# Seven products for eight in the query and forget projections of a recurrence, with the sums on GpSimd

## The chip, the core and the metric

The kernel runs on one core of one Trainium2 chip. Its engines work side by side: TensorE (PE: matrix products, with its weight loads shown apart as PEld), VectorE (DVE), ScalarE (ACT), GpSimd (POOL) and SyncE (SP, which here issues DMAs). Each executes its own instructions in the order in which they were written down, and waits for others by semaphores. SBUF is the memory of 128 partitions that they share; PSUM holds what TensorE sums, in banks of 128x512 float32. The metric is the device time of one execution, in microseconds (us).

## The reference

A decoder trunk of two layers, for 1024 tokens of width 1024, all in float32. The first layer mixes tokens by a gated linear recurrence with 8 heads of width 128; the change lies in it.

```python
q, f, i, g = jnp.split(h @ w_in, 4, axis=-1)
fg = lb + (1.0 - lb) * jax.nn.sigmoid(heads(f))
o = hgrn2_chunkwise(jax.nn.silu(heads(q)), 1.0 - fg, heads(i), jnp.log(fg))
o = o * lax.rsqrt(jnp.mean(jnp.square(o), -1, keepdims=True) + RMS_EPS)
o = o * g_norm_w.astype(jnp.float32) * jax.nn.silu(heads(g))
return o.reshape(B, S, D).astype(h.dtype) @ w_out
```

Behind it come a layer norm with the residual, a gated FFN (width 2816, a causal convolution of width 3), another norm; then the second layer with sliding-window attention in place of the recurrence, and its FFN.

## The kernel before

**Products in three parts.** Matrices are split into a high part, rounded to the format fp32r, and a low part, the rest; each product of a 128-row chunk is the sum of three matmuls of 128x512 (high x high, high x low, low x high; `mm3`, lines 194 to 196). `T` holds x transposed, high and low, 8 chunks `kc` of 128 rows by 1024 tokens. `HL` holds weights in high and low parts, 12 buffers of 1024 columns. A split is a cast on ACT (line 176) and a subtraction on DVE (line 169).

**The stages.** Up to 37.5 us x is loaded, transposed and split, and the i and g projection of head 0 is computed (lines 752, 714, 715). Then the heads follow. For each, the query and forget projection (`qf`: 4 slots, forget and query for the first 512 and the last 512 tokens, 8 chunks x 3 matmuls each, into one bank of PSUM that is read when it is full) is followed by the i and g projection (`ig_block`: 8 token blocks, 16 matmuls each). Between these matmuls stand those of the recurrence of the head before: for widths 256, 128, ... 8, DVE multiplies decays into `qp` (line 990) and `kp` (line 992) and goes on with the products of decays `tot` (line 995), and TensorE sums scores and column sums from them (line 200); ACT copies (lines 971, 977, 978, 1048, 1058). DVE's line 1184 computes, whenever the plan finds it free, differences of blocks of the FFN's down-projection weights: those two products are computed with seven block products for eight already, and their sums are stored to DRAM (`bsd`) from the buffer `Y`. The finished heads are kept in `Y` as well. From about 430 us the heads are moved to `T`, and the out projection, the norm and the FFN follow.

**What sets the order.** The recurrence stage is written out by hand for all engines. `Order` counts planned time of TensorE (`od.t`) and DVE (`od.v`). Chains of small tasks (`spawn`, `later`) are due at times of that plan: at each `tick` behind a chunk product, what is due is emitted. `lay` fills DVE's gaps: due low parts of splits, then block sums, then moves. `slot_begin` loads and stores the block sums' rows.

**Buffers.** Weights of the heads come through a ring of three raw buffers; `Y` (32 KB of each partition) serves x, block sums, heads, and later the FFN.

## Time and profile before

| | |
|---|---|
| runs (3), median | 2131.06 us (2130.61 to 2131.86) |
| profiled execution | 2131.04 us, span 2129.3 us |
| PE busy | 2119.9 us, 100% |
| DVE busy | 1760.9 us, 83% |
| ACT busy | 926.5 us, 44% |
| POOL busy | 132.5 us, 6% |
| HBM read / written | 213.94 MB / 62.94 MB |
| heads, 60 to 430 us: DMA | busy share 0.44, 152 GB/s |

A row of instructions gives line, engine, operation, output<-inputs by the program's names, the shape in partitions x elements, and a count; behind the bar stand busy time and the mean of one in ns, then the idle time of the engine just before them and who ended it. A row of a timeline starts with start and duration in us; neighbours that are alike are put together, with their count behind an x. PE's matmuls are pipelined: their durations overlap, so the spacing of starts tells what one costs.

### The profile page before, as it was taken

The numbers are of one execution on the slowest core, as the hardware profiler recorded it, in microseconds if no ns is written. First come the engines' busy times: TensorE is split into PE (matmuls) and PEld (weight loads), VectorE is DVE, ScalarE is ACT, GpSimd is POOL, SyncE is SP. The second block draws the span as 40 slices with busy tenths as digits, with TensorE's granted clock in tenths as the row PEclk, the third lists the DMA queues.
The fourth block names the chain that finished last, engine by engine and source line by source line (L and its number), as shares of the span: only waits on it lengthen the run. The fifth ranks groups of instructions, "written<-read, shape, count | busy, mean of one in ns | idle before, by whom it ended". The sixth has DMA issues, their size and how long they took to land.

```text
span 2129.3 us, 32129 instructions
## 1 busy us (share of the span) xinstructions
PE 2119.9 (100%) x12663; PEld 1779.6 (84%) x12663; DVE 1760.9 (83%) x2375; ACT 926.5 (44%) x1491; POOL 132.5 (6%) x150
## 2 busy tenths in 40 slices
PE   9999999999999999999999999999999999999998
PEld 8888888888888888888888888888888888888887
DVE  4777776677999999887988658969999999978986
ACT  4444444452444444434433356743544444444430
POOL 1000000001100000000001113321000000000002
PEclk9999999999999999999999999999999999999999
DMA  5655443214223222228854411042233222249662
GB/s 216 243 211 169 144 132 119 75 32 177 99 85 98 85 89 79 80 99 275 288 190 161 129 26 45 24 149 89 80 100 98 90 86 83 86 148 325 229 215 90
DMA packets 229838, 278.96 MB, mean 131 GB/s; under 512 B 29960, under 2 KB 158648, under 8 KB 226872
## 3 DMA queue, kind: packets, MB, share of 16 engines
q1 hardware_dynamic: 228736, 276.53, 39.0%
q8 instruction: 99, 1.62, 0.3%
q10 hardware_dynamic: 856, 0.37, 0.1%
q14 instruction: 51, 0.42, 0.1%
q0 software_dynamic: 96, 0.02, 0.0%
HBM read 213.94 MB, written 62.94 MB: 130 GB/s over the span
## 4 chain that ended last, share of the span: by engine, by line
PE 99%; DMA 0%; DVE 0%; SPq 0%; issue 0%; DVEq 0%
PE psmm L194 17%; PE psmm L196 17%; PE psmm L195 17%; PE psax L194 10%; PE psax L196 10%; PE psax L195 10%; PE psmm L714 5%; PE psax L200 4%; PE psmm L715 3%; PE psmm L204 1%; PE psmm L200 1%; PE psax L204 1%; PE psax L1427 1%; PE psmm L1274 1%; DMA Y<-in_x_dram 0%; PE psmm L752 0%
## 5 line engine op out<-in xcount | busy, mean ns | idle before, releaser
L194 PE MATMUL psmm<-T,HL 128*128 128x512 f32 x768 | 303.4, 395 | 0.0
L196 PE MATMUL psmm<-T,HL 128*128 128x512 f32 x768 | 299.4, 390 | 0.0
L195 PE MATMUL psmm<-T,HL 128*128 128x512 f32 x768 | 299.2, 390 | 0.0
L473 DVE SCALAR_TENSOR_TENSOR Y<-Y,cwt 128x1023 f32<-128x1023 f32 (+1 forms) x176 | 225.0, 1281 | 44.3 <-ACT Y L471 42.9
L221 ACT CAST HL<-rx 128x1024 fp32r<-128x1024 f32 (+1 forms) x151 | 150.7, 1007 | 178.3 <-PE psmm L195 30.9
L169 DVE TENSOR_TENSOR HL<-rx,HL 128x1024 fp32r<-128x1024 f32 (+1 forms) x151 | 178.5, 1188 | 16.9 <-ACT HL L221 16.8
L714 PE MATMUL psmm<-HL,T 128*128 128x512 f32 x496 | 176.8, 399 | 0.0
L196 PEld LDWEIGHTS psmm<-T,HL 128*128 128x128 f32 x768 | 144.2, 188 | 30.7
L194 PEld LDWEIGHTS psmm<-T,HL 128*128 128x128 f32 x768 | 144.3, 188 | 29.6 <-issue 0.4
L195 PEld LDWEIGHTS psmm<-T,HL 128*128 128x128 f32 x768 | 144.3, 188 | 28.8 <-issue 0.4
L471 ACT ACTIVATE Y<-Y,cwt 128x1024 f32<-128x1024 f32 x88 | 108.7, 1238 | 101.6 <-DVE Y L460 89.4
L715 PE MATMUL psmm<-HL,T 128*128 128x256 f32 x496 | 138.9, 280 | 0.0
L194 PE MATMUL psax<-T,HL 128*128 128x512 f32 x352 | 137.3, 390 | 0.0
L196 PE MATMUL psax<-T,HL 128*128 128x512 f32 x352 | 137.0, 389 | 0.0
L195 PE MATMUL psax<-T,HL 128*128 128x512 f32 x352 | 137.0, 389 | 0.0
L243 POOL TENSOR_TENSOR rs<-rs,nhalf 128x1 f32<-128x1 f32 x32 | 44.6, 1394 | 1286.6 <-DVE rs L242 1286.6
L714 PEld LDWEIGHTS psmm<-HL,T 128*128 128x128 f32 x496 | 93.1, 188 | 21.0
L715 PEld LDWEIGHTS psmm<-HL,T 128*128 128x128 f32 x496 | 93.7, 189 | 0.4
L221 ACT CAST HT<-rx 128x1024 fp32r<-128x1024 f32 (+1 forms) x37 | 35.5, 960 | 127.9 <-DVE rx L427 76.4
L169 DVE TENSOR_TENSOR HL<-raw,HL 128x1024 fp32r<-128x1024 f32 x51 | 62.1, 1219 | 20.2 <-ACT HL L176 19.3
L195 PEld LDWEIGHTS psax<-T,HL 128*128 128x128 f32 x352 | 66.2, 188 | 13.7
L196 PEld LDWEIGHTS psax<-T,HL 128*128 128x128 f32 x352 | 66.1, 188 | 13.6
(315 smaller groups left out, 5232.3 us busy)
## 6 DMA issues: line engine op xcount, KB each, us to landing
rx<-in_ffn_w_in_dram SPq DMA_DIRECT2D x136, 256.0 KB, 3.2
rx<-gd SPq DMA_DIRECT2D x118, 256.0 KB, 3.9
Y<-in_ffn_w_out_dram SPq DMA_DIRECT2D x44, 512.0 KB, 6.4
bsd<-Y SPq DMA_DIRECT2D x22, 1024.0 KB, 4.8
gd<-Y SPq DMA_DIRECT2D x44, 512.0 KB, 2.6
rx<-in_ffn_w_out_dram SPq DMA_DIRECT2D x54, 256.0 KB, 4.7
R<-bsd SPq DMA_DIRECT2D x44, 256.0 KB, 5.1
Y<-in_ffn_w_in_dram SPq DMA_DIRECT2D x40, 256.0 KB, 2.9
```

What stands on the lines that cost most here:

```text
L169: make = lambda e: e.tensor_tensor(lo, src, hi.bitcast(F32), op=ALU.subtract)
L194: nc.tensor.matmul(ps, st(0), mv(0), start=start, stop=False)
L195: nc.tensor.matmul(ps, st(0), mv(1), start=False, stop=False)
L196: nc.tensor.matmul(ps, st(1), mv(0), start=False, stop=stop)
L200: nc.tensor.matmul(ps, lhsT, rhs, start=start, stop=stop, **kw)
L204: nc.tensor.transpose(ps, src, ident)
L221: nc.scalar.copy(hi, src)
L243: nc.gpsimd.tensor_tensor(rs, rs, nhalf, op=ALU.pow)
L471: nc.scalar.activation(c, u, AF.Identity, bias=cwt[:, l, 3, ci:ci + 1], scale=cwt[:, l, 2, ci:ci + 1])
L473: nc.vector.scalar_tensor_tensor(c[:, sh:], u[:, :S - sh], cwt[:, l, 2 - sh, ci:ci + 1], c[:, sh:], op0=ALU.mult, op1=ALU.add)
L714: nc.tensor.matmul(ps, T[:, 0, kc, ts], w[:, :, kc % 4, :], start=kc == 0, stop=False)
L715: nc.tensor.matmul(ps[:, :256], T[:, 1, kc, ts], w[:, 0, kc % 4, :], start=False, stop=kc == KC - 1)
```

## The change

**Seven products for eight.** Of the 8 chunks of x, the first four are treated as 2x2 blocks: early and late tokens (512 each) by chunks 0-1 and 2-3. The weights are blocks of chunks 0-1 and 2-3 by query and forget. Their product takes seven block products, with four sums of x blocks and four of weights. Chunks 4 to 7 are multiplied as before. In `T`, the late tokens of chunks 0 and 1 now hold the sum of the late blocks; a new buffer `Sx` holds three more sums, high and low. Per head 90 matmuls of 128x512 stand in place of 96. Since `T` is no longer plain x there, the i and g projection takes weight differences (`us[2]`) for chunks 2 and 3 of late tokens.

**Where sums are made.** The weights' sums (line 696: four of 128x256 a head; line 685: one of 128x512), three of the four sums of x blocks at the start (lines 831 to 841, 16 operations) and the block sums of the FFN weights (line 1329, before line 1184 on DVE) run on GpSimd. The block sums go in halves of 256 columns through a new buffer `Yx`, in two chains 7.5 us apart by the plan; a load, 7 us, four differences, 4 us, a store.

**Banks.** Products that several results share stay in PSUM: the bank `pa` gets query early, forget early, forget late and query late one after the other, `pc` forget late and forget early. What stands in a bank is copied by ACT (lines 1034, 1041, 1044) or added by DVE (line 1000), and then TensorE adds to the same bank.

**Outputs through DRAM.** `Y` is allocated behind the heads now. Heads 0 to 5 are stored to `hod` and loaded into `Sx` during head 7's projection; head 6 goes to `Yx`. The out projection takes the late tokens first. Two raw buffers hold loads, the third the sums. Transposes of constants wait while a projection has all banks.

```diff
@@ qf
-            for half in range(2):
-                ts = slice(half * 512, (half + 1) * 512)
-                ps = psmm()
-                proj_T(weights["f"], half, ps)
-                nc.scalar.activation(fg[:, ts], ps, AF.Sigmoid)
...
-                proj_T(weights["q"], half, ps)
-                nc.scalar.activation(qs[:, ts], ps, AF.Sigmoid)
...
+            q, f, e = [weights[g] for g in "qfe"]
+            early, late = slice(0, 512), slice(512, 1024)
...
+            def add_on(ps, w, w0, mv, n, start=False, stop=True):
+                for k in range(n):
+                    for j, (wi, mi) in enumerate(((0, 0), (0, 1), (1, 0))):
+                        nc.tensor.matmul(ps, w[:, wi, w0 + k, :], mv(mi, k), start=start and k + j == 0,
+                                         stop=stop and k == n - 1 and j == 2, skip_group_check=True)
...
+            def plus(ts, ps):
+                nc.vector.tensor_tensor(fg[:, ts], fg[:, ts], ps, op=ALU.add)
...
+            def third(ps):
+                plus(late, ps)
...
+            pa = psmm()
+            add_on(pa, q, 0, tokens(early), 2, start=True)
+            nc.scalar.copy(qs[:, early], pa)
+            ps = psmm()
+            add_on(ps, q, 2, tokens(early, 2), 6, start=True)
+            after(1.0, query_early(ps))
+            del ps
+            yield
+            add_on(pa, e, 2, sums(0), 2)
+            nc.scalar.copy(fg[:, early], pa)
+            pc = psmm()
+            add_on(pc, f, 0, tokens(late), 2, start=True)
+            nc.scalar.copy(fg[:, late], pc)
+            pd = psmm()
+            add_on(pd, f, 4, tokens(late, 4), 4, start=True)
+            yield
+            add_on(pa, e, 0, sums(1), 2)
+            after(0.5, third(pa))
+            add_on(pc, f, 4, tokens(early, 4), 4, stop=False)
+            after(0.0, forget_late(pd))
+            del pd
+            yield
+            add_on(pc, f, 2, sums(2), 2)
+            after(0.5, forget_early(pc))
+            del pc
+            od.finish(mine[1:2])
+            add_on(pa, e, 4, tokens(late, 2), 2, stop=False)
+            add_on(pa, q, 4, tokens(late, 4), 4)
+            od.finish(mine)
+            nc.scalar.activation(qs[:, late], pa, AF.Sigmoid)
+            nc.vector.tensor_tensor(qs[:, late], qs[:, late], pa, op=ALU.mult)
@@ sums of weights
+        sub2 = nc.gpsimd.tensor_tensor
+        def ig_diff(raw):
+            d = tail["raw"][2][:, :512]
+            sub2(d, raw[:, 512:], raw[:, :512], op=ALU.subtract)
...
+        def qf_sums(q, f):
+            b11, b21, b12, b22 = q[:, :256], q[:, 256:512], f[:, :256], f[:, 256:512]
+            t3, t2, t4 = [tail["raw"][2][:, 256 * i:256 * (i + 1)] for i in range(3)]
+            for x, y, z in ((t3, b22, b12), (b12, b12, b11), (t2, b22, b12), (t4, b21, t2)):
+                sub2(x, y, z, op=ALU.subtract)
@@ block sums of the FFN weights
-                for x, y, z in ((b11, b12, b11), (b12, b22, b12), (b22, b22, b11), (b21, b21, b22)):
-                    pending.append(lambda x=x, y=y, z=z: tt(x, y, z, op=sub))
...
+            while halves:
+                i, j = halves.pop(0)
+                l, n = divmod(i, pairs)
                 for k in range(2):
+                    row = (k * pairs + n) * P
+                    nc.sync.dma_start(rows[k], part(a["ffn_w_out"][l][row:row + P, :], j))
+                yield 7.0
                 for x, y, z in ((b11, b12, b11), (b12, b22, b12), (b22, b22, b11), (b21, b21, b22)):
+                    sub2(x, y, z, op=ALU.subtract)
+                yield 4.0
+                for k in range(2):
+                    nc.sync.dma_start(part(bsd[l][:, n, k, :], j), rows[k])
+                yield 4.0
@@ heads' outputs
-            if h < NH - 1:
-                nc.scalar.activation(Y[:, h, :], ps, AF.Copy, scale=par[:, 16:17])
+            if h < NH - 2:
+                flat = og.rearrange("p c t -> p (c t)")
+                nc.scalar.activation(flat, ps, AF.Copy, scale=par[:, 16:17])
+                del ps
+                yield 2.0
+                nc.sync.dma_start(hod[:, h, :], flat)
```

**The order at the changed places.** First TensorE in the query and forget projection of head 0, which has no recurrence beside it. Before, at the change from the first slot's bank to the second's (a number behind a name tells one buffer from another):

```order
L194 MATMUL psmm_460<-T_81,HL_83 128x512
L195 MATMUL psmm_460<-T_81,HL_83 128x512
L196 MATMUL psmm_460<-T_81,HL_83 128x512
L194 MATMUL psmm_490<-T_81,HL_83 128x512
L195 MATMUL psmm_490<-T_81,HL_83 128x512
L196 MATMUL psmm_490<-T_81,HL_83 128x512
```

Each bank was filled by 24 matmuls in a row and then left. The whole projection now, where psmm_518 is `pa` and psmm_555 is `pc`:

```order
L989 MATMUL psmm_518<-T_81,HL_82 128x512 x6
L989 MATMUL psmm_528<-T_81,HL_82 128x512 x18
L989 MATMUL psmm_518<-Sx_102,HL_82 128x512 x6
L989 MATMUL psmm_555<-T_81,HL_82 128x512 x6
L989 MATMUL psmm_570<-T_81,HL_82 128x512 x12
L989 MATMUL psmm_518<-Sx_102,HL_82 128x512 x6
L989 MATMUL psmm_555<-T_81,HL_82 128x512 x12
L989 MATMUL psmm_555<-Sx_102,HL_82 128x512 x6
L989 MATMUL psmm_518<-T_81,HL_82 128x512 x18
```

The bank of the first six is entered again three times, psmm_555 once, each time behind 18 matmuls into others.

Then ScalarE in such a projection, with the recurrence of the head before beside it. Before, head 3:

```order
L900 ACTIVATE fg<-psmm 128x512
L901 ACTIVATE fg<-fg,lbt 128x512
L903 ACTIVATE kp<-fg,one 128x512
L977 COPY kd<-qp 128x32x16
L978 COPY kd<-kp 128x32x16
L907 ACTIVATE qs<-psmm 128x512
L176 CAST HL<-raw_100 128x1024
L977 COPY kd<-qp 128x8x64
```

And now, head 4, where lines 1125 and 1126 are the old 977 and 978:

```order
L1034 COPY qs<-psmm 128x512
L719 ACTIVATE sg<-VG 128x256
L1125 COPY kd<-qp 128x32x16
L1126 COPY kd<-kp 128x32x16
L1041 COPY fg<-psmm 128x512
L1013 ACTIVATE kp<-qs 128x512
L1044 COPY fg<-psmm 128x512
L1125 COPY kd<-qp 128x8x64
```

Copies out of PSUM stand where sigmoids stood, and the recurrence's copies between them as before.

Last GpSimd in the heads. Before, its rows from the start to the norm of the first head (lines 1099 and 1100, which then come once a head):

```order
L793 DMA pr<-in_hgrn_lb_logits_dram 16x128
L794 DMA pr<-in_hgrn_gnorm_w_dram 1x16x8
L169 TENSOR_TENSOR HL<-raw_99,HL 128x1024
L1099 TENSOR_SCALAR ss<-ss 128x8
L1100 TENSOR_TENSOR ss<-ss,nhalf 128x8
```

Now, from the norm of one of the last heads on (the raw buffers are raw_99 to raw_101):

```order
L1247 TENSOR_SCALAR ss<-ss 128x8
L1248 TENSOR_TENSOR ss<-ss,nhalf 128x8
L1329 TENSOR_TENSOR Yx<-Yx 128x256 x8
L696 TENSOR_TENSOR raw_101<-raw_99 128x256
L696 TENSOR_TENSOR raw_99<-raw_99,raw_100 128x256
L696 TENSOR_TENSOR raw_101<-raw_99 128x256
L696 TENSOR_TENSOR raw_101<-raw_100,raw_101 128x256
L1329 TENSOR_TENSOR Yx<-Yx 128x256 x8
L685 TENSOR_TENSOR raw_101<-raw_99 128x512
L1329 TENSOR_TENSOR Yx<-Yx 128x256 x8
```

The differences of both chains of block sums stand in groups of eight, and between them those of the projection weights.

343 lines of the change are left out of this document (215 added, 128 removed).

## The prediction

> **What bounds the kernel now.** I read the page's busy table and slices first, then the chain that ended last, then the busy time by stage, then single instructions around the work that changes.
>
> ```profile
> PE 2119.9 (100%) x12663; PEld 1779.6 (84%) x12663; DVE 1760.9 (83%) x2375; ACT 926.5 (44%) x1491; POOL 132.5 (6%) x150
> PEclk9999999999999999999999999999999999999999
> PE 99%; DMA 0%; DVE 0%; SPq 0%; issue 0%; DVEq 0%
> ```
>
> ```profile
> 0.00:37.50 37.50, 35.80 (x233) 32.74 (x234) 17.43 (x31) 16.34 (x27) 6.16 (x14) 1.00 0.57 197
> 37.50:60.00 22.50, 22.50 (x101) 18.62 (x100) 10.49 (x15) 8.93 (x13) 0.00 (x0) 1.00 0.76 277
> 60.00:430.00 370.00, 370.00 (x3817) 315.23 (x3817) 266.45 (x490) 164.61 (x370) 13.13 (x14) 1.00 0.44 152
> ```
>
> TensorE (PE) is busy for 2119.9 of the span of 2129.3 us, and the chain that ended last is PE for 99%. The second fence has one row per stretch: its length, then busy time of PE, weight loads, VectorE (DVE), ScalarE (ACT) and GpSimd (POOL), the granted clock, the DMA share and GB/s. The changed work lies in the first three stretches and the 65 us behind them. From 37.5 to 430 us PE has no idle time at all, at a clock of 1.00. So each matmul taken away there is worth its full spacing, and each wait of PE that the change makes costs its full length. DVE has 266 of 370 us of work there, ACT 165, POOL 13.
>
> **What the matmuls are worth.** These rows are of one slot of a query and forget projection; between are ten more rows, lines 194, 195 and 196 in turn.
>
> ```profile
> 301.06 0.39 PE L194 MATMUL psmm<-T,HL 128*128 128x512 f32 x1
> ...
> 303.56 0.39 PE L196 MATMUL psmm<-T,HL 128*128 128x512 f32 x1
> ```
>
> The twelve starts span 2.50 us, eleven steps of 0.227 us (the 0.39 us is latency and overlaps). Per head the two projections had 4 x 8 chunk products of 3 matmuls, 96. Of the eight block products over the first four chunks, two chunks each, one is replaced by sums; 30 chunk products are left, 90 matmuls. 8 heads x 6 = 48 matmuls fewer, and no other count on PE changes: 48 x 0.227 = **-10.9 us**. The i and g projections use other weights for the late tokens but as many matmuls. As PE was never idle there, nothing that the change removes from DVE is a further gain.
>
> **Work taken from DVE.** The sums of weight blocks for the down projection move from DVE to POOL.
>
> ```profile
> L1184 DVE TENSOR_TENSOR Y<-Y 128x512 f32<-128x512 f32 x80 | 54.6, 690 | 1.3
> L990 DVE TENSOR_TENSOR qp<-qp,tot 128x512 f32<-128x512 f32 x42 | 28.9, 688 | 25.6 <-PE psax L200 25.4
> L992 DVE TENSOR_TENSOR kp<-kp,tot 128x512 f32<-128x512 f32 x42 | 28.8, 686 | 0.0
> ```
>
> (80 of the 88 lie in this window.) 88 x 0.69 = 60.7 us leave DVE; some 35 us come back: 32 operations of 128x512 more behind the projections (additions from PSUM, line 1000, above all), 22 us, and 8 low halves of 128x768 and 8 of 128x512 of the summed weights, 13 us. DVE then works about 240 us in the 359 that are left of the stretch. That is off PE's path, cost 0; it buys the slack that is used below.
>
> **Work put on POOL.** There are 176 differences of 128x256 of the block sums, 32 of the projection weights, 8 differences of 128x512 for i and g, and 16 sums of x at the start. The nearest rows:
>
> ```profile
> L1447 POOL TENSOR_TENSOR X<-X,bf 128x512 f32<-128x512 f32 x32 | 41.1, 1286 | 54.4 <-DVE X L1439 52.6
> L478 POOL TENSOR_TENSOR Y<-Y 128x1024 f32<-128x1024 f32 x4 | 9.6, 2399 | 100.3 <-DVE Y L473 100.3
> ```
>
> 512 elements more cost 1.11 us, so 128x256 is estimated at 1286 - 557 = 0.73 us. In the heads POOL gets 208 x 0.73 + 8 x 1.29 = 162 us, 45% of the stretch; it fits. The two streams of block sums fall together in the order, so POOL runs bursts of eight, 5.8 us, about 22 times. What POOL does to DVE meanwhile is in the next rows, two pairs from the FFN:
>
> ```profile
> 606.46 2.39 POOL L478 TENSOR_TENSOR Y<-Y 128x1024 f32<-128x1024 f32 x1 [44.25 <-DVE Y L473]
> ```
> ```profile
> 606.75 2.65 DVE L428 TENSOR_TENSOR rx<-rx,Y 128x512 f32<-128x512 f32 x1
> ```
> ```profile
> L428 DVE TENSOR_TENSOR rx<-rx,Y x20: 683/686/2646, 606.8 to 1866.6; 128x512 f32<-128x512 f32 x20
> ```
> ```profile
> 1269.97 1.29 POOL L1447 TENSOR_TENSOR X<-X,bf 128x512 f32<-128x512 f32 x1
> ```
> ```profile
> 1270.36 1.28 DVE L1470 TENSOR_TENSOR Y<-psmm,tri 128x512 f32<-128x512 f32 x2
> ```
> ```profile
> L1470 DVE TENSOR_TENSOR Y<-psmm,tri x32: 674/681/692, 1259.8 to 1407.4; 128x512 f32<-128x512 f32 x32
> ```
>
> A DVE operation with both inputs in SBUF, begun 0.29 us into POOL's, took 2.65 us against a median of 0.69: it stood still until POOL was through at 608.85. The two with one input in PSUM ran in their usual time beside POOL. So each two-SBUF operation of DVE that meets a POOL difference loses up to 0.73 us. Whether that reaches PE is a question of slack, read at one step of the recurrence:
>
> ```profile
> 295.15 0.69 DVE L990 TENSOR_TENSOR qp<-qp,tot 128x512 f32<-128x512 f32 x1
> 295.75 0.69 DVE L992 TENSOR_TENSOR kp<-kp,tot 128x512 f32<-128x512 f32 x1
> ...
> 297.50 1.44 DVE L1184 TENSOR_TENSOR Y<-Y 128x512 f32<-128x512 f32 x2
> 299.68 0.69 DVE L990 TENSOR_TENSOR qp<-qp,tot 128x512 f32<-128x512 f32 x1 [0.73 <-PE psax L200]
> ```
> ```profile
> 298.97 0.67 PE L200 MATMUL psax<-qp,kp 128*32 128x32 f32 x31
> ```
>
> PE's scores of qp and kp start at 298.97; the L992 that they need ended at 296.44: 2.53 us of slack. Blocked twice (L990, L992) DVE is 1.46 us late, three times 2.19, both hidden; four times 2.92, and PE waits 0.4. In between L990 waits for PE anyway (25.6 us over 42, 0.6 each), and the L1184s are gone, two of them 1.44 us here; both pay lateness back. So most bursts should be covered. Bounds: 0, or a whole 0.73 us in each of 22 bursts, 16 us. Nearest to the step shown, where two or three blocks stay inside the slack, I take +0.1 us a burst: **+2 us**. If the cover is gone, the PE scores are late next, and with them everything behind them in PE's order.
>
> **Banks that PE enters again.** In a projection one bank of PSUM (pa, lines 1032 to 1063) holds four results one after the other and another (pc) two; ACT copies out what stands there (lines 1034, 1041, 1044), and once DVE adds it (line 1000), before PE goes on in the same bank. Between lie 18 matmuls of another bank, 18 x 0.227 = 4.1 us, four times a head. Before, no bank was needed again so soon. The lags from the end of a bank to its copy, as they stand before:
>
> ```profile
> 200.32 0.39 PE L196 MATMUL psmm<-T,HL 128*128 128x512 f32 x1
> ```
> ```profile
> 200.75 0.60 ACT L907 ACTIVATE qs<-psmm 128x512 f32<-128x512 f32 x1 [3.66 <-PE psmm L196]
> ```
> ```profile
> 133.92 0.39 PE L196 MATMUL psmm<-T,HL 128*128 128x512 f32 x1
> ```
> ```profile
> 138.13 1.65 ACT L1048 COPY A<-Ab 32x256 f32<-32x256 f32 x4
> 139.79 0.60 ACT L900 ACTIVATE fg<-psmm 128x512 f32<-128x512 f32 x1
> ```
> ```profile
> 302.45 0.68 DVE L910 TENSOR_TENSOR qs<-qs,psmm 128x512 f32<-128x512 f32 x1
> ```
> ```profile
> 296.72 0.39 PE L196 MATMUL psmm<-T,HL 128*128 128x512 f32 x1
> ```
>
> Normal is 0.20 us after the spacing of the last matmul (200.55 to 200.75). At the worst ACT came 5.64 us late (134.15 to 139.79), behind copies that wait for DVE, and DVE's read came 5.50 late (296.95 to 302.45) behind two updates. A copy of 0.6 us and a handover of 0.2 leave 3.3 us of the 4.1 for lag. The worst ACT case would cost 2.3, the DVE case 2.2. Bounds: 0, and two ACT cases and three DVE cases, 11 us. The order of the changed kernel has at most two DVE-bound copies ahead of an evacuation on ACT, and DVE's line 1000 right behind the update of width 32, with the L1184s gone: nearer to the 0.20 row. I take **+2 us**, about one late bank.
>
> **The start.** Four token blocks get sums of x before their split, 16 operations on POOL, with 4 + 1 + 4 x 0.7 us of weights: about 4 x 1.29 + 12 x 0.73 + 1.29 + 2.9 = 18 us on an engine that had 6 busy in 37.5. What PE needs soonest, the sum for the two leading chunks, is one addition on DVE and doesn't wait for POOL; the other sums are read only after the first 24 matmuls of the first projection, at 37.55 + 24 x 0.227 = 43 us. DVE had 17.4 busy, so there is room, but blocks by POOL may fall on the path. Bounds 0 and 1.7 (PE's idle time of this stretch once more); I take **+0.5**.
>
> **Edits at nothing.** The finished heads go to DRAM and back, 6 stores of 512 KB and 3 loads of 1 MB, during heads 0 to 5 and head 7: the DMA share there is 0.44, and the loads are issued a projection ahead of use. The weight rows come in 256 KB pieces, and each store of sums on SP waits for POOL; weight loads of the next head stand behind it in that queue, and they are issued one to two slots (5.4 us each) before they are split. If POOL is late by a burst of 5.8 us this cover just holds. The out projection takes the late tokens first, with the same matmuls. The constants' transposes move by a few us. Each 0, bounded by 1 us together either way.
>
> **Sum.** -10.9 + 2 + 2 + 0.5 = -6.4. The profiled execution took 2131.04 us (span 2129.3), the median of the runs 2131.06: 2131.04 - 6.4 = **2124.6 us**, 0.30% faster. About 0.2%, 4.3 us, is what a measurement of this kernel can tell from no change.
>
> **Rivals.**
>
> *All waits hidden.* For it: the slacks above, and DVE's idle time of 100 us in the heads. Against: four new re-entries a head, and POOL from 13 to 160 us. 2131.04 - 10.9 = 2120.1, to 2122.
>
> *GpSimd blocks DVE past its slack; this ends slower.* Place: the scores behind L1138 and L1140 (the old L990 and L992) while a burst of eight runs. It decides once four blocked operations come in a row without an idle gap, since 4 x 0.73 is more than 2.53. For it: with POOL and DVE in turn, DVE runs at half speed for a burst of 10 us, and low halves and gates stand between the updates. Price 0.73 us or more a burst, 16 to 22 us: 2131.04 - 10.9 + 2.5 + 16 = 2138.6.
>
> *GpSimd keeps DVE out for a whole group.* If POOL's next difference goes ahead of the waiting DVE operation, DVE stands 5.8 us and PE 5.8 - 2.5 = 3.3; at half of the bursts 36 us: 2158.6. Against: all but the first difference of a group wait for the one ahead of them, so POOL lets go between. The row at 606.75 shows one POOL operation only, so the trace does not exclude it. The Trainium skill, SBUF — State Buffer, § Who interferes with whom, says that whichever of the two starts first holds the shared pair for the whole instruction and the other fully blocks; by that, a hold ends with each instruction, which speaks for turns and for 2124.6 rather than for 2158.6. That the block lasts to the end of POOL's operation agrees with 606.75 (2.65 us); who gets the pair next no run here shows.
>
> *Late banks.* All five late cases of before come back, at 2.2 each: 2131.04 - 10.9 + 0.5 + 2 + 11 = 2133.6, no change that can be told.
>
> **Chances.** My forecast, 2122 to 2127: 0.30; all hidden 0.27; GpSimd past the slack 0.20; kept out for groups 0.10; late banks 0.13. Faster takes the first two, 0.57; same takes late banks and the milder end of the third, 0.18; slower 0.25. The range 2119.8 to 2141 leaves out the group case and the far end of the third; the forecast's own range is 2122 to 2127.
>
> **What would show it.** PE's spacing stays 0.227 us and its matmuls fall by 48. POOL's differences take 0.7 us and DVE operations with two SBUF inputs beside them up to 1.4. The waits of PE, 1.5 us before, name DVE or ACT behind lines 1034 to 1044 and 1000 (banks, 2 us) or lines 1138 and 1140 (blocks, 2 us). I am wrong if PE's waits sum to more than 7 us, if they lie at the start or the out projection, or if POOL's 128x256 takes far from 0.73.

## The result and the profile after

The changed kernel takes 2196.57 us, median of 4 runs (2193.35 to 2197.38), beside 2131.36 (2130.61 to 2131.86) for the kernel before on the same chip: a ratio of 1.0303, 95% interval 1.0286 to 1.0321. It is 65 us slower. The forecast was 2124.6 us, with a range up to 2141: wrong in sign and far outside.

The busy table and the chain that ended last, after the change:

```profile
PE 2132.0 (97%) x12615; PEld 1780.9 (81%) x12615; DVE 1804.7 (82%) x2351; ACT 952.0 (43%) x1547; POOL 368.1 (17%) x382
...
PE 84%; DVE 9%; ACT 3%; DMA 1%; issue 1%; POOL 1%; SPq 0%; DVEq 0%; ACTq 0%; POOLq 0%
```

The 48 matmuls are gone (12663 to 12615), and yet PE is busy 12.1 us longer. In a span of 2194.7 us it stands idle for 62.7, where it stood idle for 9.4 (2129.3 - 2119.9). So the account closes in three terms: waits +53.3, matmuls not issued -10.9, and +23.0 of longer busy time of the others (12.1 + 10.9); together +65.4, the difference of the spans. The chain is no longer PE alone: DVE holds 9% of it.

The stages, with the columns of the windows shown before (length, then busy time of PE, weight loads, DVE, ACT, POOL, the granted clock, DMA share, GB/s):

```profile
0.00:37.50 37.50, 34.36 (x220) 30.56 (x221) 21.22 (x38) 18.72 (x36) 26.70 (x35) 1.00 0.50 174
37.50:60.00 22.50, 22.50 (x104) 18.72 (x103) 14.88 (x19) 11.35 (x19) 9.41 (x11) 1.00 0.45 141
60.00:430.00 370.00, 336.99 (x3325) 283.40 (x3325) 271.25 (x397) 162.16 (x357) 193.44 (x190) 0.97 0.46 147
430.00:495.00 65.00, 54.63 (x540) 45.43 (x538) 43.76 (x71) 28.08 (x62) 24.66 (x28) 0.95 0.60 194
```

Before, PE had not one idle moment from 37.5 to 495; now 33 us are missing between 60 and 430 and 10 in the 65 us behind. The clock, 1.00 throughout before, is 0.97 and 0.95 on average there. What PE waited for, the largest rows (us in total, times, longest):

```profile
PE psmm L748 <- DVE HL L169: 8.2, 1, 8.2
PE psmm L989 <- DVE VG L710: 6.9, 4, 3.7
PE psmm L989 <- DVE cwt L948: 6.6, 1, 6.6
PE psax L200 <- issue: 6.2, 2, 3.5
PE psmm L204 <- DVE Y L255: 5.1, 1, 5.1
PE psmm L989 <- DVE fg L1000: 4.8, 2, 3.2
```

Most of them name DVE. In DVE's rows of the heads, 37 to 495 us, the cause that was priced at 2 us stands out (count, then shortest, median and longest in ns):

```profile
L1329 POOL TENSOR_TENSOR Yx<-Yx x176: 722/959/1794, 50.1 to 480.4; 128x256 f32<-128x256 f32 x176
...
L1140 DVE TENSOR_TENSOR kp<-kp,tot x43: 676/685/1233, 73.7 to 493.2; 128x512 f32<-128x512 f32 x43
L1140 DVE TENSOR_TENSOR kp<-kp,fg x8: 684/956/1227, 69.6 to 485.3; 128x512 f32<-128x512 f32 x8
```

A block difference on POOL takes 0.72 us when nothing is in its way, as estimated, but 0.96 in the median; in these rows DVE operations of 0.69 us take up to 1.23. Each DVE operation of this kind (`TENSOR_TENSOR`) was set against the tenth percentile of its own form: of the 284 with both inputs in SBUF, 163 overlapped one of POOL's, and together the 284 took 63.4 us too long (1.7 us before). The 102 with an input in PSUM lost 0.7 us. The typical loss of one is 0.55 us (87 of the 129 that lost over 0.1 lie between 0.5 and 0.6). What that does to PE is seen at one burst, in head 7's query and forget projection:

```profile
436.26 8.59 POOL L1329 TENSOR_TENSOR Yx<-Yx 128x256 f32<-128x256 f32 x8 [2.94 <-DMA Yx<-in_ffn_w_out_dram]
```
```profile
438.30 0.95 DVE L721 TENSOR_TENSOR VG<-VG,sg 128x256 f32<-128x256 f32 x1
439.18 1.22 DVE L1138 TENSOR_TENSOR qp<-qp,tot 128x512 f32<-128x512 f32 x1
440.33 1.21 DVE L1140 TENSOR_TENSOR kp<-kp,tot 128x512 f32<-128x512 f32 x1
441.46 0.74 DVE L1143 TENSOR_TENSOR tot<-tot 128x64 f32<-128x64 f32 x1
...
446.82 0.23 DVE L948 COPY cwt<-psmm 128x88 f32<-128x88 f32 x1
```
```profile
447.05 1.19 PE L989 MATMUL psmm<-T,HL 128*128 128x512 f32 x2 [6.56 <-DVE cwt L948]
```
```profile
447.00:452.00 5.00, 4.95 (x103) 3.88 (x103) 1.31 (x4) 0.42 (x1) 2.70 (x3) 0.50 0.70 216
```

POOL's eight differences take 8.59 us in place of 8 x 0.73. Four DVE operations in a row lose about 0.5 us each; a copy out of PSUM, which PE needs to get a bank back, stands behind them and their like, and PE stands 6.56 us. Then, in the last row, PE runs at a granted clock of 0.50.

How much of the 23 us is the clock can be read from such rows. In the changed kernel the granted clock stands at 0.50 in eight stretches of 3.41, 6.83 or 10.24 us, and PE is busy for 32.4 us in them; at half clock 16.2 us of that are lost. The other 7 us are not the clock. An estimate for a good part of them: a matmul takes 0.39 us, of which 0.16 overlap with the next one at a spacing of 0.227, and ahead of each of PE's 28 waits that overlap is missing, some 4 us. One of the eight stretches, from 496.67 to 500.08, follows a wait of only 2.13 us; the row of 495 to 500 us has it as a mean clock of 0.67:

```profile
495.42 0.50 PE L748 MATMUL psmm<-HL,T 128*128 128x512 f32 x1 [2.13 <-DVE VG L710]
```
```profile
495.00:500.00 5.00, 4.58 (x18) 3.97 (x19) 2.80 (x6) 5.00 (x9) 0.00 (x0) 0.67 0.00 0
```

Where the 65 us arise along the program, as shifts in us against before, each at the moment when PE reaches the place. The two columns beside are experiments told below: without any two-input work of POOL in the heads, and without that and three more causes.

| place in the program (us before) | changed kernel | POOL only writes | four causes off |
| --- | --- | --- | --- |
| head 0's query and forget projection (37.5) | +2.4 | +1.8 | +1.9 |
| head 1's i and g projection (85.1) | +3.8 | 0.0 | -1.0 |
| head 2's query and forget projection (114.4) | +15.7 | +10.3 | +6.6 |
| head 4's (227.2) | +34.2 | +15.5 | +9.9 |
| head 7's (398.6) | +40.3 | +11.5 | +7.5 |
| head 7's i and g projection (429.8) | +47.1 | +14.3 | +8.8 |
| out projection (489.3) | +53.7 | +21.1 | +16.1 |
| FFN, first rows (539.2) | +65.0 | +32.3 | +19.1 |
| end (2129.3) | +65.5 | +32.6 | +26.8 |

Behind the FFN's first rows the changed kernel and the second column lose next to nothing more; the third column loses another 7.7 us there, which the run on the out projection's weights explains in part.

### The profile page after: what moved, and what is told of

It reads as the page before. It is cut to its first block, busy times and chain, and to the rows that moved or that the text cites. A ratio compares the mean times of both kernels' runs of the same rounds, so it can differ in the third digit from the quotient of the medians.

```text
span 2194.7 us, 32565 instructions
## 1 busy us (share of the span) xinstructions
PE 2132.0 (97%) x12615; PEld 1780.9 (81%) x12615; DVE 1804.7 (82%) x2351; ACT 952.0 (43%) x1547; POOL 368.1 (17%) x382
## 4 chain that ended last, share of the span: by engine, by line
PE 84%; DVE 9%; ACT 3%; DMA 1%; issue 1%; POOL 1%; SPq 0%; DVEq 0%; ACTq 0%; POOLq 0%
PE psmm L194 13%; PE psmm L195 13%; PE psmm L196 13%; PE psax L194 9%; PE psax L195 9%; PE psax L196 9%; PE psmm L989 5%; PE psax L200 3%; PE psmm L200 1%; PE psmm L204 1%; PE psmm L748 1%; PE psax L1605 1%; DVE kp L1140 1%; DVE qp L1138 1%; PE psmm L1450 1%
## 5 line engine op out<-in xcount | busy, mean ns | idle before, releaser
L194 PE MATMUL psmm<-T,HL 128*128 128x512 f32 x512 | 200.5, 392 | 0.0
L196 PE MATMUL psmm<-T,HL 128*128 128x512 f32 x512 | 199.3, 389 | 0.0
L195 PE MATMUL psmm<-T,HL 128*128 128x512 f32 x512 | 199.3, 389 | 0.0
L1329 POOL TENSOR_TENSOR Yx<-Yx 128x256 f32<-128x256 f32 x176 | 173.5, 989 | 126.2 <-DMA Yx<-in_ffn_w_out_dram 104.4
L748 PE MATMUL psmm<-HL,T 128*128 128x512 f32 x496 | 181.4, 407 | 12.3 <-DVE HL L169 8.2
L169 DVE TENSOR_TENSOR HL<-rx,HL 128x1024 fp32r<-128x1024 f32 (+1 forms) x151 | 176.0, 1173 | 16.2 <-ACT HL L221 16.2
L989 PE MATMUL psmm<-T,HL 128*128 128x512 f32 x576 | 150.9, 410 | 20.2 <-DVE VG L710 6.9
L989 PEld LDWEIGHTS psmm<-T,HL 128*128 128x128 f32 x576 | 109.9, 196 | 50.5 <-issue 10.6
L196 PEld LDWEIGHTS psmm<-T,HL 128*128 128x128 f32 x512 | 96.1, 188 | 20.0
L194 PEld LDWEIGHTS psmm<-T,HL 128*128 128x128 f32 x512 | 96.1, 188 | 19.8
L195 PEld LDWEIGHTS psmm<-T,HL 128*128 128x128 f32 x512 | 96.3, 188 | 19.4
```

The costliest lines, as they stand in the source:

```text
L169: make = lambda e: e.tensor_tensor(lo, src, hi.bitcast(F32), op=ALU.subtract)
L194: nc.tensor.matmul(ps, st(0), mv(0), start=start, stop=False)
L195: nc.tensor.matmul(ps, st(0), mv(1), start=False, stop=False)
L196: nc.tensor.matmul(ps, st(1), mv(0), start=False, stop=stop)
L748: nc.tensor.matmul(ps, T[:, 0, kc, ts], w[:, :, k, :], start=kc == 0, stop=False)
L989: nc.tensor.matmul(ps, w[:, wi, w0 + k, :], mv(mi, k), start=start and k + j == 0, stop=stop and k == n - 1 and j == 2, skip_group_check=True)
```

## The experiments

The theory after the result: (1) POOL's differences block DVE's operations with two SBUF inputs, far beyond the slack, and (2) other changes of order cost as much again. The rivals: that the blocks are everything and the other waits only echo them, or that the projection's new pattern of banks is the cause.

**POOL writes, but doesn't read.** In the first run the 176 block differences become memsets of the same duration, in the same place on every engine.

```diff
-                for x, y, z in ((b11, b12, b11), (b12, b22, b12), (b22, b22, b11), (b21, b21, b22)):
-                    sub2(x, y, z, op=ALU.subtract)
+                for x in range(4):
+                    nc.gpsimd.memset(Yx[:, r, :768], 0.0)
```

> The changed kernel with each of GpSimd's 176 block-sum differences (line 1329) replaced by a memset of 128x768 into the same buffer: the same count, the same order and waits on every engine, about the same 0.73 us each, but an operation that reads nothing from SBUF (the sums of the down-projection weights are left out, so the output is not the reference's). Theory A, blocking: GpSimd operations that read SBUF hold up DVE's two-SBUF operations (63 us more DVE time than unblocked between 37 and 500 us), DVE comes late, PE waits 53 us and then runs at a lower granted clock for 23 us. Then most of both goes: DVE's excess falls to about 12 us (the 40 weight sums stay), PE's waits in the heads to under 12 us, time 2140 to 2150, of which 11 us are the wait at the out projection. Theory B, GpSimd is only late itself, or the banks and the new order make PE wait: 2185 to 2197, waits as before.

Measured: 2169.64 us (2166.69 to 2169.79), ratio 1.0176 (1.0161 to 1.0191). 27 us come back; the losses of DVE fall from 63.4 to 12.4 us. But 38 us remain, far more than theory A had left. In the next run the differences of the projection weights become memsets too, so that no POOL operation of the weights reads SBUF any more.

```diff
-            sub2(d, raw[:, 512:], raw[:, :512], op=ALU.subtract)
+            nc.gpsimd.memset(d, 0.0)
+            nc.gpsimd.memset(d, 0.0)
...
-            for x, y, z in ((t3, b22, b12), (b12, b12, b11), (t2, b22, b12), (t4, b21, t2)):
-                sub2(x, y, z, op=ALU.subtract)
+            for x in range(4):
+                nc.gpsimd.memset(tail["raw"][2][:, :768], 0.0)
```

> e1, and the 32 weight sums of 128x256 and 8 of 128x512 that the heads still make on GpSimd replaced by memsets too (these sums are left out, so the projections of q, f, i and g are not the reference's); nothing on GpSimd reads SBUF for longer than a norm's step between 60 and 490 us. e1 has 12 us of DVE excess left. If the weight sums' blocking is the next cause: excess to about 1 us, PE's waits in the heads from 26 to under 15 us, time 2148 to 2160. If what is left in e1 is the new order itself (evacuations, gates and copies in ACT's and DVE's queues): 2164 to 2170.

Measured: 2161.74 us (2160.88 to 2163.60), ratio 1.0140 (1.0123 to 1.0157). The time lies between the two ranges that were expected. DVE's losses are 1.4 us, as small as before the change, although POOL still works 159 us between 60 and 430 us (193 in the changed kernel, where its differences take longer). Groups of this run (its lines are one higher), and the largest waits that are left:

```profile
L1330 POOL MEMSET Yx<- x176: 732/740/749, 50.3 to 447.6; 128x768 f32 x176
```
```profile
L1141 DVE TENSOR_TENSOR kp<-kp,tot x48: 673/684/689, 70.2 to 482.2; 128x512 f32<-128x512 f32 x48
```
```profile
PE psmm L749 <- DVE HL L169: 6.8, 1, 6.8
PE psmm L204 <- DVE Y L255: 5.4, 1, 5.4
PE psax L200 <- issue: 3.1, 2, 2.6
```

So it is reading, not being busy, by which POOL holds DVE up: 176 memsets of 740 ns leave the longest L1141 at 689 ns. The Trainium skill, SBUF — State Buffer, § Who interferes with whom, has this: a DVE instruction with two SBUF inputs contends with a GpSimd instruction that reads SBUF, not with one that only writes it; these two runs agree (63.4 against 1.4 us). Against the changed kernel's 2196.57 the blocks are worth 35 us; by the profiles' terms 24.9 of waits (53.3 against 28.4) and 8.0 of longer busy time (23.0 against 15.0). The other 30 us, 41 with the gain counted, have other causes. In this run the gain can be seen by itself: from head 4's projection to head 7's the shift against before falls from +15.5 over +14.2 and +12.7 to +11.5, 1.2 to 1.5 us a head, where 6 x 0.227 = 1.36 were expected.

**The blocks alone.** The kernel before, with only its block differences moved from DVE to POOL; they keep their size of 128x512.

```diff
-                    pending.append(lambda x=x, y=y, z=z: tt(x, y, z, op=sub))
+                    pending.append(lambda x=x, y=y, z=z: nc.gpsimd.tensor_tensor(x, y, z, op=sub))
```

> The kernel before with one part of the change alone: the block sums of line 1184 (88 of 128x512) on GpSimd in place of DVE, at the same places of the order. Blocking: 88 operations of 1.29 us hold up DVE's two-SBUF operations; DVE loses 61 us of sums and gets 50 to 70 us of waiting in its place, but in lumps of up to 1.1 us each; PE waits 5 to 30 us and the clock falls behind some of the waits: 2140 to 2170. Rival, that GpSimd's work costs nothing by itself: 2129 to 2132.

Measured: 2177.30 us (2175.37 to 2177.57), ratio 1.0213 (1.0196 to 1.0230), above the range that was expected. The groups and the largest waits of this run:

```profile
L992 DVE TENSOR_TENSOR kp<-kp,fg x8: 687/1778/1783, 67.8 to 482.4; 128x512 f32<-128x512 f32 x8
```
```profile
L1184 POOL TENSOR_TENSOR Y<-Y x88: 1266/1616/2366, 40.2 to 425.0; 128x512 f32<-128x512 f32 x88
```
```profile
PE psmm L714 <- DVE VG L679: 10.3, 4, 4.2
PE psmm L195 <- issue: 4.3, 1, 4.3
```

Here a block costs DVE 1.1 us, twice that of a difference half as long, so DVE stands until the one difference on POOL is through. 87 blocked operations lose 72.5 us, and moving 60 us of work off DVE makes the kernel 46 us slower, with no seven-product projection in it. The 27 us of the first run, which the block differences cost in the changed kernel, and the 46 here are the price of the same move, in two orders of work and with two sizes of difference.

**Two runs that failed as experiments.** I took the waits at the out projection for a collision in the rows of the weights' buffer and rotated these rows by two, in the changed kernel and again without the block arithmetic (the second lets the block sums go as loaded).

```diff
-            return by_chunk(split_into(hl_at(4 + u), raw, eng), 4)
+            return by_chunk(split_into(hl_at(u), raw, eng), 4)
...
-            hl = split_into(hl_at(u), raw, eng)
+            hl = split_into(hl_at(u + 2), raw, eng)
```

> The changed kernel with the weight buffers of the heads rotated by two places in HL, so that the out projection's weights lie in rows 4 to 11 again, as in the kernel before; the block sums stay on GpSimd. Theory: 11 us of the loss come from SP's queue at the out projection, where the load of the norm's row (line 360) stands ahead of the last load of out-projection weights and waits 16 us for its buffer. Then PE's waits between 560 and 585 us fall from 7.8 us to under 2 and the time to about 2185. Rival: these waits are the echo of late heads; then the time stays at 2193 to 2197.

> The rotation of e2 and no block-sum arithmetic at all (loads and stores of the blocks stay; the output is not the reference's). If blocking and the out projection's queue are the whole loss but the 40 weight sums a run: 2122 to 2134, that is at or below the kernel before, PE's waits under 10 us. If the re-entered banks cost as much as the 2 to 11 us of the prediction, 5 to 10 us of waits name lines 1034, 1041, 1044 or 1000. If the new order itself is the cause: above 2160.

Measured: 2207.82 us (ratio 1.0361, 1.0346 to 1.0377) and 2172.50 (1.0196, 1.0180 to 1.0211). The premise was mistaken: the kernel before used the same rows. The rotation puts out-projection weights where the FFN's first weights are laid, so part of the out projection is computed with other weights, and a new wait of 14 us for the FFN's weights arises. The runs say nothing on the question, except that the second repeats in rough size what the block arithmetic is worth (35 us between the two).

**Banks entered again.** The first run above, and ScalarE's three copies read other data in place of the bank (the partial results in it are left out of the computation).

```diff
-            nc.scalar.copy(qs[:, early], pa)
+            nc.scalar.copy(qs[:, early], T[:, 0, 0, early].bitcast(F32))
...
-            nc.scalar.copy(fg[:, early], pa)
+            nc.scalar.copy(fg[:, early], T[:, 0, 0, early].bitcast(F32))
...
-            nc.scalar.copy(fg[:, late], pc)
+            nc.scalar.copy(fg[:, late], T[:, 0, 0, early].bitcast(F32))
```

> e1, with ACT's three copies out of the banks that PE enters again (lines 1034, 1041, 1044) reading a constant part of T in place of the bank, at the same length and the same places of the order (so the partial products are left out of q and f). PE need not wait for these copies. If re-entered banks matter beyond the waits that name them (3.1 us in e1): 2155 to 2163. If they don't: 2164 to 2170.

Measured: 2165.33 us (2161.26 to 2166.18), ratio 1.0154 (1.0139 to 1.0169), 4.3 us less than the run that it changes, with intervals that overlap. PE's waits for lines 1034 and 1044 are gone, a wait of 1.2 us for line 1000 stays. Without the block differences the copies are thus worth about 4 us or less, which these runs can't tell clearly from nothing: no main cause. In the changed kernel itself the waits that name the banks are longer, 2.1 us for line 1034, 1.6 for line 1044 and 4.8 for DVE's line 1000.

**The end of a projection.** The longest wait of the heads comes at the start of head 1's i and g projection. In the changed kernel:

```profile
88.35 0.63 ACT L1004 ACTIVATE fg<-fg 128x512 f32<-128x512 f32 x1 [2.75 <-DVE fg L1000]
...
91.99 0.72 ACT L1007 ACTIVATE kp<-fg,one 128x512 f32<-128x512 f32 x1
92.62 0.60 ACT L1125 COPY kd<-qp 128x512 f32<-128x512 f32 x1
```
```profile
93.25 0.69 DVE L1138 TENSOR_TENSOR qp<-qp,tot 128x512 f32<-128x512 f32 x1 [2.84 <-ACT kd L1125]
...
96.70 0.69 DVE L1062 TENSOR_TENSOR qs<-qs,psmm 128x512 f32<-128x512 f32 x1 [2.07 <-ACT qs L1061]
97.30 1.22 DVE L169 TENSOR_TENSOR HL<-raw,HL 128x1024 fp32r<-128x1024 f32 x1
```
```profile
98.67 0.76 PE L748 MATMUL psmm<-HL,T 128*128 128x512 f32 x1 [8.21 <-DVE HL L169]
```

With seven products three of the four results (all but the early queries) are finished in the projection's last two slots, since their banks wait for a late block product. So both gate chains (six ACT operations from 88.35 to 92.7) come at once and stand ahead of the recurrence's copies; DVE waits for a copy (2.84), then for ACT again (2.07), and the low part of the next weights, for which PE waits, is recorded behind both. Between 85 and 98 us POOL has no operation, so nothing is blocked in this stretch; with POOL only writing the wait is still 6.8 us. In the next run, the first one again, the low parts of heads 1 and 2 go two places earlier on DVE.

```diff
-            od.finish(mine)
+            [lay_low() for _ in range(len(lowparts))]; od.finish(mine)
```

> e1, with one exchange in DVE's order at two places: in heads 1 and 2 the low parts of the i and g weights (line 169) stand ahead of the last product of the projection (line 1062), not behind it. In e1 PE waits 6.8 us at 89 us for such a low part; line 1062 itself waits 2.1 us for ACT there. If the place behind line 1062 is the cause, the wait falls to about 3 to 4 us and the time by 3 to 5 us with the clock behind it, to 2164 to 2167; if the operation ahead (line 1138, waiting for ACT's copies of kd behind six gate operations) is, the wait stays above 4.5 us and the time within 2 us of e1.

Measured: 2164.55 us (2163.72 to 2166.26), ratio 1.0155 (1.0140 to 1.0171): 5.1 us less, and the wait is 4.1 in place of 6.8. The order at the end of a projection is a cause of its own; the edit mends a part of it.

**The clock behind a wait.** Is the lower clock an effect of the waits? The kernel before got seven pauses of PE, at the head of the projections, by memsets on POOL of rising number.

```diff
+        def pause(h, ps):
+            touch = lambda: nc.tensor.matmul(ps[:32, :16], hold[:, :32], hold[:, :16], start=True, stop=True)
+            touch()
+            for _ in range((0, 6, 12, 19, 27, 38, 52, 72)[h]):
+                nc.gpsimd.memset(hold, 0.0)
+            touch()
```

> The kernel before, with seven pauses of PE by design: ahead of the projections of heads 1 to 7 PE makes a tiny product, GpSimd 6, 12, 19, 27, 38, 52 and 72 small memsets behind it (about 0.16 us each), and PE a second tiny product that waits for them. Pauses of about 1, 2, 3, 4.5, 6, 8.5 and 12 us, 37 us in all. If a pause costs only its length: 2131 + 37 = 2168 and matmul spacings of 0.227 us behind every one. If the clock falls behind pauses, as it does in the changed kernel (granted clock 0.50 in the 5 us behind a wait of 6.6 us): 2 to 4 us more for each pause above some length, 2175 to 2190, with doubled spacings for some us behind it.

Measured, one run: 2195.57 us, beside 2131.56. The pauses (1.31, 2.57, 4.04, 5.71, 8.01, 10.95 and 15.13 us) sum to 47.7, more than the 37 planned; the total rose by 64.0. The pause of 4.04 and what came behind it:

```profile
182.15 0.24 PE L895 MATMUL psmm<-hold 128*32 128x16 f32 x2 [4.04 <-POOL hold L898]
...
183.03 0.63 PE L196 MATMUL psmm<-T,HL 128*128 128x512 f32 x1
183.46 0.63 PE L194 MATMUL psmm<-T,HL 128*128 128x512 f32 x1
...
186.52 0.39 PE L196 MATMUL psmm<-T,HL 128*128 128x512 f32 x1
186.75 0.40 PE L194 MATMUL psmm<-T,HL 128*128 128x512 f32 x1
```
```profile
119.00:125.00 6.00, 5.62 (x29) 4.70 (x30) 5.52 (x11) 1.65 (x3) 0.27 (x2) 1.00 0.24 91
```

Matmuls start every 0.43 us until 186.02, 3.7 us long, then every 0.23 again; behind the pause of 2.57 us (the last row: 119 to 125 us) the clock stayed at 1.00. The two short pauses cost 0.6 us each beside themselves, for the tiny products and the handovers; each pause from 4.04 up costs 2.2 to 3.2, and the longest no more than that of 8.01. The Trainium skill, TensorE: Matmul & The Clock Gate, Part 1: The HAM clock gate, says that an idle window of about 3.4 us halves the clock, and as long a busy one brings it back. The pauses agree, and so do the lengths of the slow stretches (3.41 us and multiples of it). The changed kernel's waits of 2.13 and 2.78 us, each with a stretch at half clock behind it, don't agree with a limit of 3.4 us, and there the measurement decides. So the 16 us at half clock in the changed kernel are a second price of its waits, the shorter ones too.

**The out projection's weights.** On SP's queue, before and after (start, duration of the issue):

```profile
485.21 8.17 SPq L164 DMA_DIRECT2D rx<-in_hgrn_w_out_dram  x3
...
508.33 0.34 SPq L360 DMA_DIRECT2D HL<-gd  x1
```
```profile
561.70 0.33 SPq L360 DMA_DIRECT2D HL<-gd  x1
562.13 0.84 SPq L164 DMA_DIRECT2D rx<-in_hgrn_w_out_dram  x2
```

Line 360 loads what has to be stored first, and waits for it. Before, the last weights of the out projection (line 164) were issued ahead of it; now they stand behind it until 562.13, with the out projection running since 543.0. The next run is the first one with the loads recorded as urgent, which puts all of them ahead of line 360.

```diff
-                    out_late(late, rows, n, ff.TX)
+                    with urgent(): out_late(late, rows, n, ff.TX)
```

> The kernel with memsets for the block sums (block sums left out of the computation), with one more edit: the out projection's second stage is recorded as urgent, so that on SP's queue all loads of its weights (line 164) stand ahead of the load at line 360, which waits for the sum of the attention outputs; DVE's order moves there too. Theory A (the waits of PE between 560 and 590 us come from weights that stand on SP behind line 360): the waits at lines 255 and 221 (5.3 and 1.6 us) go, and the clock with them: 8 to 11 us less than that kernel's 2169.6, 2159 to 2162. Theory B (the out projection waits for DVE, which is late from the heads): the waits stay or move to other lines, 2167 to 2172.

Measured: 2167.27 us (2165.57 to 2168.69), ratio 1.0168 (1.0152 to 1.0183), only 2.4 us less, with ranges that overlap: the time is theory B's. At the place theory A holds: the out projection's own loss falls from 11.2 us (from +27.3 to +38.5) to 3.1 (from +25.6 to +28.7), and its wait for line 255 from 5.3 to 1.6. But 5.6 us are lost again behind it, in the FFN, where the runs so far had lost nothing:

```profile
645.82 2.40 POOL L478 TENSOR_TENSOR Y<-Y 128x1024 f32<-128x1024 f32 x1 [4.56 <-DVE Y L473]
```
```profile
646.16 3.14 DVE L169 TENSOR_TENSOR HL<-rx,HL 128x1024 fp32r<-128x1024 f32 x1
...
653.34 1.21 DVE L169 TENSOR_TENSOR HL<-Y,HL 128x1024 fp32r<-128x1024 f32 x1
```
```profile
654.61 0.67 PE L196 MATMUL psmm<-TX,HL 128*128 128x512 f32 x1 [3.28 <-DVE HL L169]
```

An old POOL operation of the FFN meets a low part on DVE (3.14 us in place of 1.22), and PE waits 3.28 us for another low part, five operations later, then runs at half clock. The block is not all of it: in the first run a low part is blocked there too (2.84 us, at 652.31), but it is the one that PE needs, it stands ahead of the other, and PE doesn't wait. So the edit also changed DVE's order in the FFN, and how much of the 3.28 us is the order and how much the block was not tried. Neither theory had that.

**All of it together.** First with the four causes taken away in one kernel, memsets for all weight sums, then the two edits of order in the changed kernel with its whole computation.

```diff
+                    with urgent(): out_late(late, rows, n, ff.TX)
...
+            [lay_low() for _ in range(len(lowparts))]; od.finish(mine)
...
+                    nc.gpsimd.memset(Yx[:, r, :768], 0.0)
...
+            nc.scalar.copy(qs[:, early], T[:, 0, 0, early].bitcast(F32))
```

> All four single edits in one kernel: memsets in place of the block sums and the weight sums on GpSimd, ScalarE's copies from the banks that are entered again replaced by copies of other data, the low parts of the weights two places earlier, and the out projection's loads ahead of line 360 (block sums, weight sums and the partial results left out). Theory A (the causes are separate places and add): 2161.7 of the kernel without any POOL sums, less about 4, 5 and 9 us: 2141 to 2147. Theory B (they are one lateness that shows at whatever place is weakest): little more than the largest of them, 2150 to 2156. In both it stays slower than the kernel before (2131), since the waits at the constants' transposes, at the start and in the projections' last slots are left.

> The changed kernel with its whole computation, only with the low parts two places earlier in heads 1 and 2 and the out projection's loads ahead of line 360. Theory A (separate places, so what they bring without the block sums they bring with them too): 2196.6 - 5 - 9 = 2179 to 2185. Theory B (beside the blocked operations of DVE another wait takes their place): 2189 to 2197. Slower than before in either case.

Measured: 2157.50 us (ratio 1.0120, 1.0105 to 1.0135) and 2193.36 (1.0286, 1.0269 to 1.0303). That is theory B, in the first even above its numbers: three edits that had measured 4, 5 and 2.4 us alone bring 4.2 together without POOL's reads. The two edits of order bring 3.2 beside those reads, where the ranges of the runs overlap with the changed kernel's. In the second the wait at head 1 falls from 8.2 to 5.5 us, but the waits of the next heads take its place, and at head 3's i and g projection the kernel is as late as without the edit (+30.5 against +29.7); the FFN's wait is there again with 3.4 us.

**The constants' transposes.** In the changed kernel a transpose of the FFN's constants took the bank for which PE waited 6.56 us. Two runs move the four transposes: the first all behind head 7, the second some 10 us later; in each the order on PE and DVE is otherwise as it was.

```diff
-            yield 330.0
+            yield 400.0
```

> The changed kernel with its whole computation; the four transposes of the FFN's constants (line 947, copied by DVE in line 948) come behind head 7's i and g projection, all other instructions of PE and DVE stand in the same order. Theory A (one of these transposes takes a bank of PSUM just before head 7's projection, and its copy on DVE stands behind blocked operations, so that PE waits 6.6 us for the bank and then runs some us at half clock): the wait at line 948 is gone and the start of head 7's i and g projection comes 7 to 10 us earlier against the kernel before; 2196.6 becomes 2187 to 2190. Theory B (DVE is late there anyway, and the projection waits for another of its results): a wait of 3 to 6 us for line 710, 1140 or 1000 stands in its place, 2192 to 2197.

```diff
-                yield 10.0
+                yield 20.0 if l == 0 else 10.0
```

> The changed kernel with its whole computation; the transposes of the constants come some 10 us later and so behind the end of head 7's query and forget projection, their loads nearly where they were. Theory A (the bank that the first transpose takes, with its copy behind blocked operations of DVE, costs its wait of 6.6 us and 1 to 3 us of half clock): no wait for line 948 above 1 us, no new wait for the loads, 2196.6 becomes 2187 to 2190. Theory B (DVE is late there, and another of its results is waited for later): head 7's i and g projection begins 7 us earlier, as in the run before, but the out projection does not: 2193 to 2198.

Measured: 2201.04 us (2199.55 to 2203.66; ratio 1.0332, 1.0315 to 1.0350) and 2192.53 (2191.11 to 2198.07; 1.0296, 1.0279 to 1.0313). In both head 7's i and g projection begins earlier, by 7.1 and 5.7 us. The first edit moved the constants' loads with the transposes, which I had not meant, and pays for it:

```profile
505.38 0.38 PE L947 MATMUL psmm<-ident,cr 88*128 88x88 f32 x1 [7.02 <-DMA cr<-in_ffn_conv_w_dram]
```

In the second run 5.4 us of span last to the end, 4.0 by the medians, between the two theories and with ranges that overlap with the changed kernel's. The wait of 6.56 us is gone, but those for line 1140 have grown from 2.5 to 5.8 us, and one of 2.3 for line 948 has come at another place, which theory A excluded.

A last run has all three edits of order in the changed kernel, with its whole computation.

```diff
+                    with urgent(): out_late(late, rows, n, ff.TX)
...
+            [lay_low() for _ in range(len(lowparts))]; od.finish(mine)
...
+                yield 20.0 if l == 0 else 10.0
```

> The changed kernel with its whole computation and the three edits of order together: low parts two places earlier, the out projection's loads ahead of line 360, the constants' transposes later. Theory A (they add): 2193.4 of the first two, less 7 to 10 us: 2183 to 2187. Theory B (lateness of DVE moves on to the next wait): 2190 to 2196. Slower than before in either case, since the blocked operations stay.

Measured: 2189.90 us (2187.54 to 2191.24), ratio 1.0274 (1.0259 to 1.0290), at the edge of theory B: 6.7 of 65 us. No version of the changed kernel tried here comes near the kernel before: even with POOL's reads and the copies from banks taken out and two edits of order in, 26 us are left. Whether an order made anew for seven products would do better was not tried. The kernel before stays the fastest.

## Why the prediction was wrong

- **Matmuls, -10.9.** Right: 48 fewer, and 1.2 to 1.5 us a head where nothing else disturbs.
- **Work taken from DVE, cost 0.** The amount was right: 233 us of DVE work in 370 without blocks, where the forecast's 240 in 359 would be 247. The conclusion from it was not. DVE has time enough in sum, but its work lies in an order that was fitted to the old pattern of results.
- **Work put on POOL, +2: this step failed first.** The mechanism was read rightly from one row of the FFN, and the operation's own time too (0.73). What failed is "two or three blocks stay inside the slack". POOL's bursts of eight last 8.6 to 10.3 us, not 5.8, because blocks hold up POOL as well; in the burst shown four DVE operations in a row are blocked and two more soon behind them, the very point that the rival named as decisive. And the slack of 2.53 us was read at one step, between updates and scores; it was not looked up for the copies out of PSUM, the gates and the low parts that stand in the same queue. Measured: 63.4 us lost by DVE, about 33 us of the time by the spans (35 by the medians), where the forecast had 2 and its rival 16 to 22.
- **GpSimd keeps DVE out for a whole group.** Refuted: the losses cluster at 0.5 to 0.6 us, the longest is 1.09, so DVE gets its turn between two of POOL's operations. In the kernel before with 128x512 differences the loss is 1.1. The Trainium skill, SBUF — State Buffer, § SBUF: two separate sides, says that whichever of the two starts first gets the shared pair for the whole instruction; these sizes fit it, since the loss is twice as large beside a difference twice as long.
- **Banks, +2.** The right size without the block differences: about 4 us or less. With them the waits that name the banks sum to 8.5 us, 4.8 of them for a DVE operation that comes late.
- **The start, +0.5.** Measured +2.4, of which +1.8 is there without POOL's weight differences.
- **"Each 0, bounded by 1 us together": this step failed second.** The out projection "takes the late tokens first, with the same matmuls", but its loads went behind line 360 on SP, a queue that this sentence did not follow: 11.2 us are lost there in the first run, 8.1 less with the loads ahead. "The constants' transposes move by a few us", into the middle of a projection that needs its banks: a wait of 6.56 us, of which 4 to 5 us come back when they move, at the edge of what the runs can tell.
- **Not in the sum at all.** Three of four results that finish at the end of a projection, and with them two gate chains at once: up to 8.2 us of wait at head 1, and 10 us of the shift there without any block (0.0 to +10.3). And the clock: a sum of waits was taken as the price of the waits, but of the 76 us lost 16 are half clock behind them.
- **Chances.** Slower had 0.25, and its worst case was 2158.6. Every rival was one cause; that one order which is disturbed in five places gives five waits was not among them.

Open is how the rest divides. With the four causes off, 37.7 us are still lost beside the gain (26.8 + 10.9): 23.8 in waits, the longest 4.1 at head 1 and 3.9 in the FFN, and 13.9 in longer busy time. Which of these waits would stay if the others went was not tried. The seven-product projection with its block differences left on DVE was not tried either, though it is the nearest rival to the change: DVE's 233 us of work in 370 without blocks leave room in sum for their 60.

## What to carry to other kernels

Before moving elementwise work from VectorE to GpSimd, count the VectorE operations with two SBUF inputs that will run beside it: here each lost 0.55 us beside a 128x256 difference and 1.1 beside one of 128x512, and 60 us of work taken away cost 46. Where TensorE had no idle time, a term that saves 11 us must be set against the smallest slack of every queue that it reorders, not against a typical one, and each wait of some 4 us, or even of 2 to 3, can count some 2 us more for the clock. When one wait is mended, look at once for the next one: edits that measured 2 to 5 us each alone measured 4 together.

## What the runs showed of the hardware that I had not expected

- A wait may be repaid at less than full speed: behind pauses from 4.04 us up PE ran at half clock, for 3.7 us behind the shortest of them; behind 2.57 it did not. But in the changed kernel it did so behind waits of 2.13 and 2.78 us, and not behind one of 2.08. What decides it for short waits is open.
- Blocks hurt both sides: POOL's 128x256 went from 0.72 to 0.96 us in the median.
- PE stood still inside a run of equal matmuls, with no semaphore to wait for:

```profile
207.73 0.69 PE L200 MATMUL psax<-qp,kp 128*32 128x16 f32 x61
211.89 0.18 PE L200 MATMUL psax<-qp,kp 128*32 128x16 f32 x1 [3.47 <-issue]
```
```profile
q8 instruction: 1, 0.02, 1.3%
```

In the stretch from 207.5 to 212 us one packet of instructions was moved, while data kept the DMA engines nearly full for its first half. That suggests that PE waited for its code, but no run shows it. The changed kernel lost 6.2 us in two such waits, the kernel before with its differences on POOL 4.3 and 2.2, and the kernel before none above 0.1. Why a later PE meets them and an undisturbed one doesn't is not settled.
